# A two-layer transformer step on one core: the first chunks behind each later norm multiply an operand without the token's factor

## The chip, the cores and the metric

The kernel runs on one core of a Trainium2 chip. The metric is the device time of one execution in microseconds; 2365.01 us is the median of three runs before the change. A change of 2% of that is 47 us.

## The reference

One step of a backbone with two layers. Two groups of 128 tokens, a prompt and a sample, go through the same weights, so the kernel works on 256 token columns. Every layer has a mixer and a gated feed-forward part with a convolution over positions, each behind a norm whose output is modulated:

```python
for l in range(DEPTH):
    mod = silu(cond) @ w_ada[l] + b_ada[l]
    sh1, sc1, gt1, sh2, sc2, gt2 = split(mod, 6)
    h = rmsnorm(x, g_norm_mix[l]) * (1 + sc1) + sh1
    m = mixer_ab(h, ...) if l % 2 == 0 else mixer_c(h, ...)   # h @ w_in, attention, @ w_out
    x = x + gt1 * m
    h = rmsnorm(x, g_norm_ffn[l]) * (1 + sc2) + sh2
    x = x + gt2 * conv_ffn(h, w_ffn_up[l], ...)               # h @ w_up, conv, silu, @ w_down
return rmsnorm(x, g_final), ...

def rmsnorm(x, g):
    return x * rsqrt(mean(x * x, axis=-1) + EPS) * g
```

The norm divides every token by one factor of that token, taken over all 2048 features. The scale `(1 + sc) * g` and the shift `sh` belong to a feature and a group. So `h @ W` can also be written as the token's factor times `(x * scale) @ W`, plus `sh @ W`.

## The kernel before, in words

x lies in SBUF with the features on the partitions: 16 pieces (`KD`) of 128 features by 256 tokens. A product is computed in chunks of 128 output features. `gemm` (L330) runs one chunk: for each of the 16 blocks k three matmuls of a rounded float32 type, high weights by high operand, high weights by low operand, low weights by high operand, 128 by 128 by 256, summed in one PSUM bank. The operand lies as two halves of 256 columns, high part and rest, in one tile `hx`. The weights come as 1 MB tiles per chunk of 16 blocks; `split` (L243) makes the high part with a cast on ScalarE (L244) and the rest with a subtraction on VectorE (L245). There are three buffers for tiles, four for eight split blocks each, and three PSUM banks for sums (`pacc`).

Four norms stand ahead of products; this text is on the three later ones, ahead of the up-projection of layer 0, the input projection of layer 1 and the up-projection of layer 1. In the prediction they are seams A, B and C. Ahead of each runs a product whose chunks are added to x by `residual` (L653, L656 on VectorE): the output projection of layer 0, the second half of the down-projection of layer 0 (chunks of 22 blocks), the output projection of layer 1. Each residual is squared on ScalarE (L196) and added up on GpSimd (L200).

At the seam `modulated` (L613) does this in order. `stat_rstd` (L220) sums the squares over the features with four small matmuls, VectorE adds epsilon (L208), GpSimd raises to -0.5 (L211). `diagonal` (L231) and `spread` (L235) bring the factor to all partitions with one matmul against ones. `modulate` (L583) makes the operand in 16 pieces: x times factor on VectorE (L596), scale and shift of one group on VectorE (L602) and of the other on ScalarE (L605), the cast to the high half on ScalarE (L606), the rest on VectorE or GpSimd (L591). With `fixed` (seams B and C) this order is pinned and every fourth rest goes to VectorE, otherwise every second. `first_three` (L309) then runs three chunks at once while the pieces come, with an interleaved order of matmuls. The chunks behind them run one by one.

The modulation vectors themselves are products with `w_ada`, spread over the whole run in units of 512 outputs: row units on TensorE (`sum_rows`, L463, four groups of matmuls from four `araw` tiles of 1 MB), side units on VectorE (`sum_block`, L481, sixteen steps of two instructions from `block` tiles of 256 KB) and feature units on VectorE (L452). The lists `ROWS` and `BESIDE` say which unit goes where, `RATE`, `SIDE` and `FRATE` how many steps follow each chunk (`pump`, L553). In seam A, B and C one row unit is done within the seam. `ada_finish` (L389) turns the sums into columns.

Instructions that `keep_order` names are pinned to the order in the program; a planner places the others by its own costs. DMAs are issued by SyncE in one queue.

## Time and profile before

| | us |
|---|---|
| median of three runs | 2365.01 |
| lowest, highest | 2364.16, 2393.71 |
| profiled execution | 2362.85 |
| its span in the profile | 2361.1 |
| TensorE busy | 2306.7 (98%) |
| VectorE busy | 1847.8 (78%) |
| ScalarE busy | 1164.5 (49%) |
| GpSimd busy | 175.7 (7%) |

PE is TensorE's matmuls, PEld its weight loads, DVE VectorE, ACT ScalarE, POOL GpSimd, SP SyncE, whose queue issues the DMAs. A row of a timeline gives start and duration in us, engine, line and operation, output and inputs by the names of the program, shape and count, and in brackets the idle time before it with what ended it. A row of groups gives, behind the shape and the count, the busy time in us, the mean of one in ns, and the idle time before them. A float32 matmul that is not of the rounded type leaves two records.

### The profile page before, as it was taken

The numbers are of one execution on the slowest core, as the hardware profiler recorded it, in microseconds if no ns is written. First come the engines' busy times: TensorE is split into PE (matmuls) and PEld (weight loads), VectorE is DVE, ScalarE is ACT, GpSimd is POOL, SyncE is SP. The second block draws the span as 40 slices with busy tenths as digits, with TensorE's granted clock in tenths as the row PEclk, the third lists the DMA queues.
The fourth block names the chain that finished last, engine by engine and source line by source line (L and its number), as shares of the span: only waits on it lengthen the run. The fifth ranks groups of instructions, "written<-read, shape, count | busy, mean of one in ns | idle before, by whom it ended". The sixth has DMA issues, their size and how long they took to land. (4 is left out here: it accounts for less than half of the span.)

```text
span 2361.1 us, 47623 instructions
## 1 busy us (share of the span) xinstructions
PE 2306.7 (98%) x19624; PEld 2183.2 (92%) x19624; DVE 1847.8 (78%) x2822; ACT 1164.5 (49%) x1857; POOL 175.7 (7%) x210
## 2 busy tenths in 40 slices
PE   6999999999999999999999999999999999999997
PEld 4778768899999999999989999998999999999997
DVE  3569866779999999999878888798899755666654
ACT  4245544465553355554464444446555534555543
POOL 0002202100000000001220000022000000000011
PEclk9999999999999999999999999999999999999999
DMA  9988888667777877777768888777677555555553
GB/s 368 360 310 283 310 316 328 248 241 251 261 265 285 303 268 260 262 259 274 285 249 279 306 295 312 249 242 271 245 260 258 198 194 197 197 195 191 192 193 124
DMA packets 108249, 612.96 MB, mean 260 GB/s; under 512 B 11712, under 2 KB 19584, under 8 KB 40832
## 3 DMA queue, kind: packets, MB, share of 16 engines
q1 hardware_dynamic: 108032, 609.92, 71.3%
q8 instruction: 154, 2.52, 0.4%
q14 instruction: 63, 0.52, 0.1%
HBM read 605.12 MB, written 4.75 MB: 258 GB/s over the span
## 5 line engine op out<-in xcount | busy, mean ns | idle before, releaser
L104 PE MATMUL acc<-hx,wh 128*128 128x256 f32 x8416 | 1456.3, 278 | 9.3 <-ACT hx L606 4.4
L104 PEld LDWEIGHTS acc<-hx,wh 128*128 128x128 f32 x8416 | 1272.6, 188 | 46.8 <-issue 16.6
L244 ACT CAST wh<-raw 128x1024 fp32r<-128x1024 f32 (+1 forms) x822 | 795.3, 978 | 943.1 <-PE acc L104 759.7
L245 DVE TENSOR_TENSOR wl<-raw,wh 128x1024 fp32r<-128x1024 f32 (+1 forms) x822 | 923.8, 1141 | 315.6 <-ACT wh L244 310.4
L104 PE MATMUL acc<-hx,wl 128*128 128x256 f32 x4208 | 1167.6, 278 | 2.5 <-DVE wl L245 2.3
L104 PEld LDWEIGHTS acc<-hx,wl 128*128 128x128 f32 x4208 | 790.7, 188 | 20.1 <-issue 7.1
L104 PE MATMUL acc<-g,wh 128*128 128x256 f32 x2816 | 478.8, 276 | 0.0
L104 PEld LDWEIGHTS acc<-g,wh 128*128 128x128 f32 x2816 | 423.4, 188 | 0.0
L104 PE MATMUL acc<-g,wl 128*128 128x256 f32 x1408 | 388.0, 276 | 0.0
L452 DVE CUSTOM_DVE_ANT_0 junk<-araw,condb 128x2048 f32<-128x2048 f32 x120 | 274.7, 2289 | 0.0
L104 PEld LDWEIGHTS acc<-g,wl 128*128 128x128 f32 x1408 | 264.2, 188 | 0.0
L481 DVE SCALAR_TENSOR_TENSOR aacc<-block,condw,aacc 128x512 f32<-128x512 f32 x270 | 199.0, 769 | 9.3 <-DMA block<-w_ada 9.0
L200 POOL TENSOR_TENSOR sqacc<-sqacc,sq 128x256 f32<-128x256 f32 x62 | 91.3, 1472 | 1507.6 <-issue 1210.6
L1127 ACT ACTIVATE cv<-acc,convw 128x256 f32<-128x256 f32 x176 | 98.2, 558 | 5.1 <-PE acc L104 5.1
L104 PE MATMUL acc<-oall,wh 128*128 128x256 f32 x512 | 90.3, 281 | 1.8 <-DVE oall L245 1.1
L104 PE MATMUL ada<-araw,condw 128*32 128x512 f32 (+1 forms) x608 | 77.4, 591 | 13.6 <-DMA araw<-w_ada 13.0
L656 DVE SCALAR_TENSOR_TENSOR x<-acc,mod,x 128x128 f32<-128x128 f32 x192 | 58.1, 343 | 39.6 <-PE acc L104 39.6
L1130 DVE SCALAR_TENSOR_TENSOR cv<-acc,convw,cv 128x254 f32<-128x254 f32 x176 | 83.6, 475 | 6.1 <-ACT cv L1127 6.1
L1133 DVE SCALAR_TENSOR_TENSOR cv<-acc,convw,cv 128x254 f32<-128x254 f32 x176 | 84.4, 479 | 3.6
L104 PEld LDWEIGHTS acc<-oall,wh 128*128 128x128 f32 x512 | 78.4, 191 | 2.7 <-DVE oall L245 1.3
L104 PE MATMUL acc<-oall,wl 128*128 128x256 f32 x256 | 71.4, 280 | 0.0
L196 ACT ACTIVATE sq<-x 128x256 f32<-128x256 f32 x75 | 31.0, 415 | 36.2 <-DVE x L656 32.4
(194 smaller groups left out, 1273.7 us busy)
## 6 DMA issues: line engine op xcount, KB each, us to landing
raw<-w_up SPq DMA_DIRECT2D x176, 1024.0 KB, 4.8
araw<-w_ada SPq DMA_DIRECT2D x142, 1024.0 KB, 5.8
raw<-w_down SPq DMA_DIRECT2D x88, 1024.0 KB, 4.8
raw<-w_in_c SPq DMA_DIRECT2D x48, 1024.0 KB, 6.6
block<-w_ada SPq DMA_DIRECT2D x144, 256.0 KB, 5.2
raw<-w_in_ab SPq DMA_DIRECT2D x19, 1024.0 KB, 6.1
raw<-w_out_ab SPq DMA_DIRECT2D x16, 1024.0 KB, 7.4
raw<-w_out_c SPq DMA_DIRECT2D x16, 1024.0 KB, 6.9
```

Of the source, the lines that this page charges most:

```text
L104: return self.placed(nc.tensor.matmul(*a, **kw))
L196: act.activation(sq, src, AF.Square)
L200: eng.tensor_tensor(out=st["acc"], in0=st["acc"], in1=sq, op=ALU.add)
L244: pin(act.copy(out_hi, src))
L245: pin(dve.tensor_tensor(out=out_lo, in0=src, in1=out_hi.bitcast(F32), op=ALU.subtract))
L452: keep_order(dve.tensor_tensor_reduce(out=T_(feat["pool"], [P, D], "junk"), in1=feat["row"][:, c], in0=feat["raw"].rearrange("p g n -> p ( ...
L481: i = dve.scalar_tensor_tensor(out=acc[c], in0=block, scalar=condw[:, k, c:c + 1], in1=acc[c], op0=ALU.mult, op1=ALU.add)
L656: dve.scalar_tensor_tensor(out=x[:, c, s], in0=ps[:, s], scalar=mod[:, l, 3 * which + 2, c, g:g + 1], in1=x[:, c, s], op0=ALU.mult, op1=AL ...
L1127: pin(act.activation(y, ps, AF.Identity, scale=cw[:, 1, m:m + 1], bias=cw[:, 3, m:m + 1]))
L1130: pin(dve.scalar_tensor_tensor(out=y3[:, :, 1:], in0=p3[:, :, :T - 1], scalar=cw[:, 0, m:m + 1], in1=y3[:, :, 1:], op0=ALU.mult, op1=ALU.add))
L1133: pin(dve.scalar_tensor_tensor(out=y3[:, :, :T - 1], in0=p3[:, :, 1:], scalar=cw[:, 2, m:m + 1], in1=y3[:, :, :T - 1], op0=ALU.mult, op1=A ...
```

## The change

At the three later norms the first chunks no longer wait for the token's factor.

- While x is completed, `raw_rows` writes x times the scale, high part and rest, into a second operand tile `u`. The shift of the two groups stands beside them as two more columns (`raw_shift`), so a row is 258 wide (`UW`).
- `modulated` runs three chunks on `u`. The statistics run in the middle of chunk 0, the spread early in chunk 1, the four groups of row sums in chunks 1 and 2. `scaled` multiplies a chunk's sums in PSUM by the factor and adds the shift's column.
- The modulated operand `hx` is still made, for all later chunks, between chunk 0 and chunk 3.
- At seam C there is no row unit any more: unit (1, 5, 0) goes to the side units, (1, 3, 3) from these to the row units of the attention stage, and a fourth chunk runs on `u`, in the bank `misc`. The side units of layer 1 begin in head 0 and run at 1.4 steps per chunk of the output projection.
- `modulate` is no longer pinned. The matmuls of the chunks on `u` are.
- The operand tiles change places: seam A has `u` in a pool of its own, B and C swap between `keep` and `cc`. `o_all` moves to `keep`.

```diff
-SHIFT = 448
+SHIFT = 320
-ROWS += [(1, 2, 1), (1, 2, 2), (1, 2, 3), (1, 4, 0), (1, 3, 0)]
-ROWS += [(1, j, q) for j in (4, 3) for q in (1, 2, 3)]
+ROWS += [(1, 2, 1), (1, 2, 2), (1, 2, 3), (1, 4, 0), (1, 3, 0), (1, 3, 3)]
+ROWS += [(1, 4, 1), (1, 4, 2), (1, 4, 3), (1, 3, 1), (1, 3, 2)]
-RLIMIT = {"ab": 17, "ffn0": 21, "c": 26, "ffn1": 33}
+RLIMIT = {"ab": 17, "ffn0": 21, "c": 27, "ffn1": 33}
-BESIDE = {0: [17, 18, 19], 1: [26, 27, 28, 29, 30, 31]}
-SIDE = {"in3": 0.6, "heads": 1.05, "out0": 0.9, "c": 1.7, "outc": 2.0}
+BESIDE = {0: [17, 18, 19], 1: [27, 28, 29, 30, 31, 32]}
+SIDE = {"in3": 0.6, "heads": 1.05, "out0": 0.9, "c": 1.7, "outc": 1.4}
+UW = NT + 2
...
-    def gemm(blocks, xh, xl, n=NT, first=0, between=None):
-        fixed = lambda i: keep_order(i) if between else i
-        ps = T_(pacc, [P, 512], "acc")
+    def gemm(blocks, xh, xl, n=NT, first=0, between=None, ps=None):
+        fixed = lambda i: keep_order(i) if between is not None else i
+        ps = ps if ps is not None else T_(pacc, [P, 512], "acc")
...
-            if between and i == (last + 1) // 2:
-                between()
+            if callable(between):
+                if i == (last + 1) // 2:
+                    between()
+            elif between and i in between:
+                between[i]()
...
+    def raw_rows(u, l, which):
+        at = [0]
+        def row(c):
+            for g in range(2):
+                s = slice(g * T, (g + 1) * T)
+                act.activation(u[:, c, s], x[:, c, s], AF.Identity, scale=scl[:, l, which, c, g:g + 1])
+            for g in range(2):
+                s = slice(g * T, (g + 1) * T)
+                dve.scalar_tensor_tensor(out=u[:, c, UW + g * T:UW + (g + 1) * T], in0=x[:, c, s],
+                                         scalar=scl[:, l, which, c, g:g + 1],
+                                         in1=u[:, c, s].bitcast(F32), op0=ALU.mult, op1=ALU.subtract)
+        def behind(c):
+            for _ in range(2 if c < KD - 1 else KD):
+                if at[0] > c:
+                    break
+                if c == KD - 1:
+                    ensure(l, 3 * which + 1)
+                elif (l, 3 * which + 1, at[0] // 4) not in done:
+                    break
+                row(at[0])
+                at[0] += 1
+        return behind
...
-    def modulated(st, l, which, W, fixed):
+    def modulated(st, l, which, W, u, to):
         ensure(l, 3 * which + 1)
         ensure(l, 3 * which)
         while later:
             later.pop(0)()
+        for q in range(4):
+            raw_shift(u, l, which, q)
...
-        raws = [load_tile(0), load_tile(1)]
-        hx = T_(keep, [P, KD, ROW], "hx", F32R)
-        r = stat_rstd(st, D, att_bank)
-        sum_rows(0, raws[0], bank())
-        rb = spread(diagonal(r, (0, 1)), bank=att_bank)
-        sum_rows(1, raws[1])
-        raws += [load_tile(2), load_tile(3)]
-        modulate(hx, rb, l, which, range(KD), fixed)
...
-        ps = first_three(W, lambda k: hx[:, k, :NT], lambda k: hx[:, k, NT:2 * NT],
-                         AS_MADE if fixed else IN_TURN, lambda: sum_rows(2, raws[2]), fixed)
-        W.ahead(lambda i: i)
-        return hx, ps, [last_rows, turn]
+        def sums(t):
+            sum_rows(t, raws[t], bank() if t == 0 else None)
+            if t < 2:
+                load_tile()
+        hooks = [{8: stats}, {2: factor}, {}]
+        if unit:
+            load_tile()
+            load_tile()
+            hooks[1][8] = lambda: sums(0)
+            hooks[1][14] = lambda: sums(1)
+            hooks[2][5] = lambda: sums(2)
+            hooks[2][11] = lambda: sums(3)
+        uh, ul = (lambda k: u[:, k, :UW]), (lambda k: u[:, k, UW:])
+        ps = [gemm(W.chunk(), uh, ul, UW, between=hooks[c]) for c in range(2)]
+        last = W.chunk()
+        rb = got["rb"]
+        rbs = T_(tmp, [P, NT], "sq", bufs=2)
+        act.copy(rbs, rb)
+        hx = operand(*to)
+        for p in ps:
+            scaled(p, rbs)
+        for c in range(0, KD, 4):
+            modulate(hx, rb, l, which, range(c, c + 4))
+            if c in (4, 8):
+                W.ahead(lambda i: i)
+        ps.append(gemm(last, uh, ul, UW, between=hooks[2]))
+        scaled(ps[2], rbs)
...
+        else:
+            ps.append(gemm(W.chunk(), uh, ul, UW, between={}, ps=bank()))
+            scaled(ps[3], rbs)
+        return hx, [p[:, :NT] for p in ps], todo
+
+    def scaled(p, rb):
+        b = T_(small, [P, 2], "shift")
+        act.copy(b, p[:, NT:UW])
+        dve.tensor_tensor(out=p[:, :NT], in0=p[:, :NT], in1=rb, op=ALU.mult)
+        two = lambda v: v.rearrange("p (g t) -> p g t", g=2)
+        dve.tensor_tensor(out=two(p[:, :NT]), in0=two(p[:, :NT]),
+                          in1=b[:, :, None].to_broadcast([P, 2, T]), op=ALU.add)
...
             residual(gemm(W.chunk(), oh, ol, first=8), l, 0, c, st)
+            rows(c)
             pump(RATE["out0"] if c < KD - QUIET[1] else 0)
...
+            if h == 0:
+                side_start("c", BESIDE[1], cp, True)
...
                     residual(ps, l, 1, c, st if q == NQ - 1 else None)
+                    if rows:
+                        rows(c)
```

More of the change, by code (lines that the diff above doesn't have):

```diff
@@ L406, in copy @@
             n = NT if on_dve else 512
-            am = T_(tmp, [P, 512], "am", bufs=1)
+            if acc is None:
+                am = T_(tmp, [P, 512], "am", bufs=1)
+            else:
+                am = T_(side["pool"], [P, NT], "amside", bufs=1)
             act.copy(am[:, :n], got["ps"][:, :n])
@@ L611, in modulate, with raw_shift, home, operand @@
             low(c, h)
-    def modulated(st, l, which, W, fixed):
+    def raw_rows(u, l, which):
[20 more added lines that the diff above has]
+        return behind
+    def raw_shift(u, l, which, q):
+        k = slice(4 * q, 4 * q + 4)
+        sh = mod[:, l, 3 * which, k]
+        act.copy(u[:, k, NT:UW], sh)
+        dve.tensor_tensor(out=u[:, k, UW + NT:], in0=sh, in1=u[:, k, NT:UW].bitcast(F32), op=ALU.subtract)
+    def home(pl, tag):
+        return T_(pl, [P, (KD * 2 * UW + 127) // 128 * 128], tag, F32R)
+    def operand(pl, tag):
+        return home(pl, tag)[:, :KD * ROW].rearrange("p (k n) -> p k n", k=KD)
+    def raw_tile(pl, tag):
+        return home(pl, tag)[:, :KD * 2 * UW].rearrange("p (k n) -> p k n", k=KD)
+    def modulated(st, l, which, W, u, to):
         ensure(l, 3 * which + 1)
@@ L619, in modulated @@
             later.pop(0)()
+        for q in range(4):
+            raw_shift(u, l, which, q)
         if which:
             ada["i"] += len(BESIDE[l])
-        u = ROWS[ada["i"]]
-        tile_ = lambda t: T_(wpool, [P, 4, 512], "araw", bufs=2)
-        def load_tile(t):
-            raw = tile_(t)
-            sp.dma_start(out=raw, in_=A["w_ada"][u[0], u[1], u[2], t])
-            return raw
-        raws = [load_tile(0), load_tile(1)]
-        hx = T_(keep, [P, KD, ROW], "hx", F32R)
-        r = stat_rstd(st, D, att_bank)
@@ L650, in modulated, with load_tile, stats, factor @@
-        W.ahead(lambda i: i)
-        return hx, ps, [last_rows, turn]
+        unit = ROWS[ada["i"]] if ada["i"] < len(ROWS) else None
+        raws, got = [], {}
+        def load_tile():
+            raw = T_(wpool, [P, 4, 512], "araw", bufs=2)
+            sp.dma_start(out=raw, in_=A["w_ada"][unit[0], unit[1], unit[2], len(raws)])
+            raws.append(raw)
+        def stats():
+            got["r"] = stat_rstd(st, D, att_bank)
+            got["dg"] = diagonal(got["r"], (0, 1))
+        def factor():
+            got["rb"] = spread(got["dg"], bank=att_bank)
@@ L957, in mixer_ab, with out_ab @@
                 flush()
+        return o
+    def out_ab(o, st, u):
+        l = 0
+        rows = raw_rows(u, l, 1)
         ensure(l, 2)
@@ L1096, in mixer_c @@
         ensure(l, 2)
+        u = raw_tile(cp, "hxc")
+        rows = raw_rows(u, l, 1)
         W = Weights(A["w_out_c"], KD, 1)
@@ L1135, in conv @@
                                              op0=ALU.mult, op1=ALU.add))
-                if early:
+                if early and ready:
                     W.ahead(pin)
@@ L1158, in down @@
             def down(gs, q):
+                u, rows = None, None
+                if q == NQ - 1 and l < NL - 1:
+                    u = raw_tile(keep, "hx")
+                    rows = raw_rows(u, l + 1, 0)
                 for c in range(KD):
@@ L1187, in step_kernel @@
         half_unit(0, 0, first[0], keep_order)
-        hx = T_(keep, [P, KD, ROW], "hx", F32R)
+        hx = operand(keep, "hx")
         st = stat_init()
         with tc.tile_pool(name="beside", bufs=1) as beside:
-            mixer_ab(hx, rb0, st, beside)
-        W = Weights(A["w_up"][0], KD, 1)
-        hx, ready, todo = modulated(st, 0, 1, W, False)
+            o = mixer_ab(hx, rb0, beside)
+            with tc.tile_pool(name="raw", bufs=1) as rp:
+                T_(rp, [P, SHIFT // 4], "pad")
+                u = raw_tile(rp, "u")
+                out_ab(o, st, u)
+                W = Weights(A["w_up"][0], KD, 1)
+                hx, ready, todo = modulated(st, 0, 1, W, u, (keep, "hx"))
     stage[0] = "ffn0"
     st = stat_init()
-    ffn(hx, W, ready, todo, 0, st)
+    u = ffn(hx, W, ready, todo, 0, st)
     stage[0] = "c"
@@ L1200, in step_kernel @@
         ppool["att"] = ppool["ada"]
+        T_(cp, [P, SHIFT // 4], "pad")
         W = Weights(A["w_in_c"], KD, 1)
-        hx, ready, todo = modulated(st, 1, 0, W, True)
+        hx, ready, todo = modulated(st, 1, 0, W, u, (cp, "hxc"))
         load_cw(1)
```

32 lines of the change are left out of this document (17 added, 15 removed).

## The prediction

> **What bounds the kernel now.** I read the page's first part, then TensorE's waits to find the places where it stops, then a table by stretches over those places.
>
> ```profile
> span 2361.1 us, 47623 instructions
> PE 2306.7 (98%) x19624; PEld 2183.2 (92%) x19624; DVE 1847.8 (78%) x2822; ACT 1164.5 (49%) x1857; POOL 175.7 (7%) x210
> ...
> core 0: us, PE busy (x) PEld busy (x) DVE busy (x) ACT busy (x) POOL busy (x), PEclk, DMA share, GB/s
> 455.30:485.21 29.91, 24.18 (x182) 19.21 (x182) 22.60 (x59) 19.11 (x47) 8.05 (x9) 0.94 0.56 212
> 1188.85:1217.00 28.15, 25.02 (x181) 19.34 (x179) 22.52 (x52) 19.66 (x45) 9.88 (x13) 0.94 0.71 259
> 1613.75:1643.85 30.10, 26.34 (x191) 19.86 (x191) 24.87 (x57) 20.97 (x49) 12.74 (x14) 0.94 0.70 280
> ```
>
> TensorE is busy 98% of the span, so only what it does not do can be won. The three stretches reach from the last matmul of the output projection (of down for the second) to the end of the third chunk of the next weights: seams A, B and C, one behind each later norm. Only there, and at the start and the end of the kernel, is PE's busy time well below the stretch, and the granted clock (the column behind POOL) falls to 0.94. To price them I need TensorE's full pace and what it must do there in any case.
>
> ```profile
> 1180.92 0.39 PE L104 MATMUL acc<-g,wh 128*128 128x256 f32 x2
> 1188.40 0.39 PE L104 MATMUL acc<-g,wh 128*128 128x256 f32 x2
> 1188.74 0.28 PE L104 MATMUL att<-cst,sqacc 128*128 128x1 f32 x2
> 1190.67 0.38 PE L104 MATMUL att<-cst,sq 128*128 128x1 f32 x2 [1.65 <-ACT sq L196]
> 1193.33 1.22 PE L104 MATMUL att<-diag,cst 128*128 128x256 f32 x2
> 1196.03 0.85 PE L104 MATMUL acc<-hx,wh 128*128 128x256 f32 x2 [0.38 <-ACT hx L606]
> 1206.48 1.06 PE L104 MATMUL misc<-araw,condw 128*32 128x512 f32 x8
> ```
>
> This is TensorE's timeline at seam B. From 1180.92 to 1188.40 lie 66 matmuls: 0.1133 us each, the full pace. The seam's three chunks are 144 matmuls, 16.3 us. Beside them run three groups of row sums for the modulation (four matmuls each, 1.06 us by the row at 1206.48), 3.2 us. So 19.5 us are work, and A loses 29.91 - 19.5 = 10.4 us, B 8.65, C 10.6. In C 0.64 us more is work:
>
> ```profile
> 1613.73 0.64 PE L104 MATMUL misc<-aacc,cst 128*32 128x256 f32 x8
> ```
>
> That is **29 us in all**, the ceiling of this change. The loss in B: the square of the last chunk of x, waited for until 1190.67; the factor's chain until the spread over the partitions at 1193.33; the first modulated chunk, not there before 1196.03; then TensorE follows the modulation. The other two show the same waits:
>
> ```profile
> PE att L104 <- ACT sq L196: 2.9, 1, 2.9
> PE acc L104 <- DVE cv L1133: 1.0, 1, 1.0
> ```
> ```profile
> PE att L104 <- POOL sqacc L200: 2.0, 1, 2.0
> ```
>
> The first two rows are A's, the third is C's.
>
> **The change, part by part.** It removes the wait ahead of the first chunk: chunks 0 to 2 (in C 0 to 3) multiply x times the scale, ready before the norm, and the token's factor is put to the sums. The statistics run in the middle of chunk 0, the spread early in chunk 1. All PE instructions of these chunks are pinned in this order, so whatever a hook waits for holds up every matmul behind it. I take t0 as the seam's start.
>
> *Two more columns.* 480 matmuls (ten chunks of 48) become 258 wide.
>
> ```profile
> 310.53 0.51 PE L104 MATMUL acc<-kv_in,wh 128*128 128x384 f32 x2
> 312.09 0.51 PE L104 MATMUL acc<-kv_in,wh 128*128 128x384 f32 x2
> ```
>
> Nine matmuls of 384 columns take 1.56 us here, 0.173 each; against 0.1133 that is 0.47 ns a column, so two columns cost 0.9 ns and all of them **0.45 us**. No row shows a width of 258 or a start off a round address. Lower bound 0 (more columns give no gain); upper bound the row at 1193.33, a float32 product not rounded, 1.15 us until the next start: 480 x 1.04 = 500 us. I take the 384-wide row, which has the type of these matmuls.
>
> *Raw rows.* Per seam 32 ACT scalings and 32 DVE subtractions of 128x128, issued behind the residuals of the stage before.
>
> ```profile
> L656 DVE SCALAR_TENSOR_TENSOR x<-acc,mod,x 128x128 f32<-128x128 f32 x192 | 58.1, 343 | 39.6 <-PE acc L104 39.6
> L605 ACT ACTIVATE nt<-nt,mod,scl 128x128 f32<-128x128 f32 x64 | 29.6, 489 | 14.9 <-DVE nt L596 13.3 <-DVE mod L377 1.5
> L845 DVE TENSOR_TENSOR proj<-proj,acc 128x256 f32<-128x256 f32 x44 | 17.9, 417 | 24.4 <-PE acc L104 24.4
> L1130 DVE SCALAR_TENSOR_TENSOR cv<-acc,convw,cv 128x254 f32<-128x254 f32 x176 | 83.6, 475 | 6.1 <-ACT cv L1127 6.1
> ```
>
> By the nearest rows that is 32 x 0.489 = 15.6 us of ACT and 32 x 0.343 = 11 us of DVE. Whether they hide is read from the stages that get them (out projection, down, out projection of layer 1):
>
> ```profile
> 372.00:455.30 83.30, 83.18 (x713) 75.50 (x713) 60.06 (x93) 34.98 (x53) 19.80 (x14) 1.00 0.82 303
> 1068.50:1188.85 120.35, 120.35 (x1065) 120.35 (x1063) 106.97 (x131) 53.58 (x74) 24.63 (x14) 1.00 0.72 268
> 1518.70:1613.75 95.05, 93.26 (x803) 91.99 (x801) 87.81 (x138) 42.75 (x75) 23.37 (x18) 0.98 0.74 245
> ```
>
> DVE is idle for 23, 13 and 7 us of them, ACT for 48 or more. In the third, side sums move out: their number stays (six units of 16 steps, one exchanged for another), but they begin two products earlier at 1.7 steps each and then run at 1.4 instead of 2.0 per chunk, so of some 26 steps 96 - 44 x 1.7 = 21 stay.
>
> ```profile
> L481 DVE SCALAR_TENSOR_TENSOR aacc<-block,condw,aacc 128x512 f32<-128x512 f32 x52 | 43.4, 853 | 0.0
> ```
>
> 52 instructions in 43.4 us make 1.7 us a step, 8 us less, so DVE's idle time there stays near 5 us. I book 0.5 us for these stages; bounds 0 and all of 3 x 11 us.
>
> *Start of chunk 0.* Its rows are there but the last, which follows the last residual and is wanted 45 matmuls (5.1 us) after t0. Weights: in A
>
> ```profile
> 449.98 1.14 ACT L244 CAST wh<-raw 128x512 fp32r<-128x512 f32 x2 [1.53 <-PE acc L104]
> 456.18 2.18 ACT L244 CAST wh<-raw 128x512 fp32r<-128x512 f32 x4 [4.74 <-DMA raw<-w_up]
> ```
>
> the casts up to 449.98 are before t0 = 455.3; the one at 456.18, held by a transfer, is for the third tile, wanted 12 us later. I book nothing; were it the first, 2.5 us.
>
> *Statistics and spread.* The statistics come 26 matmuls in, at t0 + 2.95. The square was there at t0 + 1.8 in B, 0.5 us late for this in A by the wait above (2.9 us), on time in C. From the first statistic on the square to the spread B took 2.66 us, while the spread is now due only 56 matmuls in, at 6.35 plus about 0.8 for the statistics: t0 + 7.2, no wait. The two hooks cost TensorE 2.0 us.
>
> *Row sums.* Four groups stand in chunks 1 and 2 of A and B, 4.24 us, work moved and not added. Tiles 2 and 3 are loaded only when sums 0 and 1 have released their buffers: issued about t0 + 11.7, used at 17.1.
>
> ```profile
> araw<-w_ada SPq DMA_DIRECT2D x142, 1024.0 KB, 5.8
> ```
>
> With 5.8 us to land that is 0.4 us late; it hides behind the next part. In C the fifth unit moves into the attention stage, where its four groups cost the same 4.24 us.
>
> *Chunk 3 still needs the modulated operand.* This sets the seam's end.
>
> ```profile
> 1192.55 0.48 DVE L231 TENSOR_SCALAR diag<-cst,rr 128x128 f32<-128x128 f32 x2 [0.81 <-POOL rr L211]
> 1194.59 0.42 DVE L596 TENSOR_TENSOR nt<-x,att 128x256 f32<-128x256 f32 x1 [1.56 <-PE att L104]
> 1213.69 0.74 POOL L591 TENSOR_TENSOR hx<-nt,hx 128x256 fp32r<-128x256 f32 x1 [0.66 <-ACT hx L606]
> ```
>
> In B the factor was used first 1.26 us after the spread began; in the new order that is t0 + 8.4. The modulation then took from 1194.59 to 1214.43, 19.84 us. What filled it:
>
> ```profile
> L602 DVE TENSOR_SCALAR nt<-nt,scl,mod 128x128 f32<-128x128 f32 x16 | 8.4, 522 | 0.5
> L605 ACT ACTIVATE nt<-nt,mod,scl 128x128 f32<-128x128 f32 x16 | 7.9, 492 | 4.4 <-DVE nt L596 4.4
> L596 DVE TENSOR_TENSOR nt<-x,att 128x256 f32<-128x256 f32 x16 | 6.6, 413 | 1.6 <-PE att L104 1.6
> L245 DVE TENSOR_TENSOR wl<-raw,wh 128x512 fp32r<-128x512 f32 x6 | 3.9, 681 | 0.0
> ```
>
> DVE's groups come to 18.9 us with six weight splits (3.9), ACT's activation alone to 7.9 and its cast to nearly as much: the modulation is a chain over both engines that can't be compressed much. Now two splits fewer fall into it (-1.3), but the convolution of chunk 0 (2 x 0.475, not in B) and two scalings of PSUM with two instructions each (nearest row the 0.417 us add from PSUM: 0.83 each). The last of the 16 pieces is ready at 8.4 + 19.84 - 1.3 + 0.95 + 1.67 = t0 + 29.5. TensorE ends chunk 2 at 16.3 + 2.0 + 4.24 = 22.55 and wants that piece at 27.65. It waits 1.9 us, and chunk 3 ends at **t0 + 29.9**. Before, chunk 3 ended 5.44 us of matmuls and one group of sums behind the window: 36.4 in A, 34.65 in B. The gains are **6.5 and 4.75 us**.
>
> In C four chunks run ahead (24.4 us with the hooks and the 0.64). One more scaling and a split (0.65 x 2) shift the last piece to about 31.6; chunk 4 ends at 32.0, with the moved sums and the 0.64 booked 36.9, where before it was 30.10 + 1.06 + 10.88 = 42.0. Gain **5.1 us**. The sum is 16.35 - 0.45 - 0.5 = **15.4 us**. The profiled execution took 2362.85 us beside its span of 2361.1, so it would take 2347.45; the median of the runs, 2365.01, lies 2.2 us higher, so the forecast is **2349.5 us**.
>
> The granted clock may matter here: three windows of about 29 us at 0.94 are worth 1.7 us each, though no recorded wait exceeds 2.9 us. The Trainium skill, "TensorE: Matmul & The Clock Gate", section "What's actually happening", gives half rate after one idle window of about 3.4 us. By it the remaining waits of 2 us would cost no clock, as in my sum; by the rows a wait of 1.65 us among thin matmuls was enough in B, and the sum would fall by up to 5 us.
>
> **The rivals.**
>
> *Clean (17%).* The modulation keeps pace because its order is free and half of its last steps go to each of DVE and POOL. Then chunk 3 ends at 28.0 in A and B and chunk 4 at 34.1 in C: gains 8.4 + 6.65 + 7.9 - 0.45 = 22.5, **2342.5 us**. Against it: DVE and ACT fill B's window.
>
> *PSUM takes the place of the norm (17%).* Three accumulators hold chunks 0 to 2; the next chunk needs chunk 0 scaled and convolved. These instructions stand behind the modulation in the program. If they are also run there, chunk 3 of A starts at about t0 + 31 and ends at 36.5 (gain 0), chunk 4 of C at 43.4 with the moved sums (-1.4); B empties its sums by ACT and keeps its 4.75. Gain 3, **2362 us**. For it: A's wait of 1.0 us for a convolution.
>
> *Slower: the raw rows come ahead of weight splits (13%).* DVE pays 0.69 us per row in front of the splits that feed TensorE. It decides where a stage's DVE has less slack than its 11 us, which C's comes near. If every row is seen, 33 us against 15.4: **2382.6 us**.
>
> *258 columns don't run at the rounded type's pace (3%).* By the upper bound 2365 + 500 = **2865 us**.
>
> **How the numbers follow.** The forecast has 50% (2346 to 2353). From 2340 to 2366 lie that, most of the clean case, the PSUM case and the mild end of the slow one: about 82%. Two per cent, about what a measurement of this kernel can tell from no change, is 47 us: more than the 29 that there are to win, and more than the slow rival costs. So faster by over 2% gets 0.01, slower 0.03 (the last rival), within 2% 0.96.
>
> **What would show it.** Right: at t0 no wait of TensorE, the first matmul on x times the scale within 1 us of it; granted clock about 1.00 in the seams; the wait in chunk 3 (C: 4) on the modulated operand, 2 us; 258-wide matmuls at 0.114 us; DVE busy 11 us more in the stages before. Wrong: a wait on a convolution or a scaling ahead of chunk 3 or 4; waits on weight splits inside out projection or down; a hook that holds the pinned matmuls for the square, or for an araw tile, by more than 1 us.

## The result: 8 us slower, where 15 us less had been forecast

| | before | after |
|---|---|---|
| median | 2364.44 us (22 runs) | 2372.71 us (22 runs) |
| lowest, highest | 2361.22, 2393.71 | 2368.76, 2424.22 |
| profiled execution | 2362.85 | 2369.62 |

The ratio is 1.0066, with a 95% interval of 1.0044 to 1.0087. The forecast was 2349.5 us and its range ended at 2366: the sign was wrong, and the time lies outside the range, though within the 2%. Times of this kernel also jump by some 26 us at once (9 of the 22 runs after lie near 2397 or 2424, one of the 22 before at 2394), by a second pace of TensorE that the last section shows; without these runs the medians are 2364.31 and 2371.79 us, 7.5 us apart.

Counting the same matmuls in both traces gives where the change came in. The products stand in the same order, so matmul number k of one answers to number k of the other. A stretch of a seam reaches from the last matmul of the product ahead of it to the last one of the sixth chunk behind it.

| stretch | forecast, us | measured, us |
|---|---|---|
| up to seam A | 0 | -3.1 |
| seam A | -6.5 | -0.9 |
| seam B | -4.75 | +1.5 |
| attention and output projection of layer 1, with the moved unit | +4.24 | +4.6 |
| seam C | -9.3 | +4.2 |

The first row is scatter: 2.9 of its 3.1 us lie ahead of the stage that makes the raw rows of A, where no work was changed, and the product matmul at that mark (number 1512 of the list) starts between 324.2 and 328.6 us in the seventeen traces of this study. The stage with the moved unit comes out near its forecast. The three seams do not. (C's forecast is its gain of 5.1 with the moved 4.24 counted apart.)

The first part of the page and a table by stretches, both of the kernel after:

```profile
span 2367.8 us, 47881 instructions
PE 2311.2 (98%) x19624; PEld 2192.5 (93%) x19624; DVE 1881.7 (79%) x2960; ACT 1194.8 (50%) x1980; POOL 151.6 (6%) x202
...
core 0: us, PE busy (x) PEld busy (x) DVE busy (x) ACT busy (x) POOL busy (x), PEclk, DMA share, GB/s
369.10:452.40 83.30, 83.30 (x717) 75.99 (x715) 72.31 (x127) 45.46 (x87) 14.11 (x14) 1.00 0.77 288
452.38:475.99 23.61, 23.61 (x189) 19.44 (x187) 19.77 (x55) 16.33 (x42) 5.74 (x7) 1.00 0.71 266
475.99:479.66 3.67, 0.00 (x1) 0.03 (x1) 3.67 (x12) 3.63 (x9) 0.88 (x2) 0.88 1.03 404
479.66:485.55 5.89, 5.89 (x27) 5.89 (x28) 5.05 (x10) 4.46 (x11) 1.62 (x2) 0.50 0.96 380
1066.00:1184.64 118.64, 118.64 (x1049) 118.64 (x1048) 114.22 (x163) 61.61 (x108) 17.48 (x14) 1.00 0.74 270
1184.64:1209.30 24.66, 23.69 (x191) 19.65 (x190) 20.52 (x54) 17.34 (x45) 4.54 (x5) 1.00 0.87 310
1517.30:1615.90 98.60, 97.82 (x827) 93.25 (x825) 88.49 (x159) 53.42 (x109) 21.21 (x18) 1.00 0.75 259
1615.90:1620.67 4.77, 0.10 (x2) 0.02 (x2) 4.77 (x11) 1.88 (x5) 0.00 (x0) 0.81 0.53 206
1620.67:1629.10 8.43, 7.52 (x35) 6.08 (x35) 3.21 (x10) 0.61 (x2) 0.71 (x1) 0.50 0.35 124
1654.31:1659.90 5.59, 5.59 (x26) 5.55 (x27) 5.00 (x11) 5.04 (x11) 1.91 (x2) 0.51 0.78 284
```

PE's share of the span is as before, and so little help. The stretches tell it. The rows 369.10 and 1066.00 are the stages that make the raw rows of A and B: 83.30 us as before, and no idle time of PE in either; DVE is busy for 12 and 7 us more there (forecast 11). Seam A begins as drawn up, 23.61 us without an idle moment at full clock. Then PE stands still for 3.67 us, with DVE and ACT busy throughout, and behind that the clock is at 0.50 for 5.89 us. In C the stop comes ahead of everything (1615.90), the clock is low for 8.43 us, and it happens again at 1654.31.

TensorE's timeline at A, B and C:

```profile
452.38 0.49 PE L105 MATMUL acc<-u,wh 128*128 128x258 f32 x2
456.58 0.40 PE L105 MATMUL acc<-u,wh 128*128 128x258 f32 x2
459.82 0.40 PE L105 MATMUL acc<-u,wh 128*128 128x258 f32 x2
475.71 0.28 PE L105 MATMUL acc<-u,wl 128*128 128x258 f32 x1
479.66 0.77 PE L105 MATMUL acc<-hx,wh 128*128 128x256 f32 x2 [3.67 <-ACT wh L245]
...
1203.16 1.07 PE L105 MATMUL misc<-araw,condw 128*32 128x512 f32 x8 [0.97 <-DMA araw<-w_ada]
1214.79 0.38 PE L105 MATMUL acc<-hxc,wh 128*128 128x256 f32 x1 [1.24 <-DVE hxc L599]
1218.20 0.39 PE L105 MATMUL acc<-hxc,wh 128*128 128x256 f32 x1 [2.27 <-DVE hxc L599]
...
1620.67 0.59 PE L105 MATMUL att<-cst,sq 128*128 128x1 f32 x2 [4.67 <-ACT sq L197]
1625.09 0.78 PE L105 MATMUL acc<-hxc,wh 128*128 128x258 f32 x2
1654.31 0.76 PE L105 MATMUL acc<-hx,wh 128*128 128x256 f32 x2 [3.75 <-ACT wh L245]
```

VectorE's and ScalarE's timelines around these waits:

```profile
479.04 0.47 DVE L1230 SCALAR_TENSOR_TENSOR cv<-acc,convw,cv 128x254 f32<-128x254 f32 x1
...
1207.78 0.85 DVE L758 TENSOR_TENSOR rope<-dev,cst 64x256 f32<-64x256 f32 x2
1211.24 1.22 DVE L246 TENSOR_TENSOR wl<-raw,wh 128x1024 fp32r<-128x1024 f32 x1
1212.71 0.57 DVE L1074 SCALAR_TENSOR_TENSOR nlam<-ex 128x1 f32<-128x1 f32 x1
1213.20 0.87 DVE L486 TENSOR_SCALAR aacc<-block,condw 128x512 f32<-128x512 f32 x2
1218.75 0.41 DVE L599 TENSOR_TENSOR hxc<-nt,hxc 128x256 fp32r<-128x256 f32 x1
...
1616.45 0.61 DVE L633 SCALAR_TENSOR_TENSOR hxc<-x,scl,hxc 128x128 fp32r<-128x128 f32 x2
1616.97 1.28 DVE L246 TENSOR_TENSOR wl<-raw,wh 128x512 fp32r<-128x512 f32 x2
1618.18 1.40 DVE L489 SCALAR_TENSOR_TENSOR aacc<-block,condw,aacc 128x512 f32<-128x512 f32 x2
1619.51 0.60 DVE L743 SCALAR_TENSOR_TENSOR x<-acc,mod,x 128x128 f32<-128x128 f32 x2
1653.68 0.48 DVE L1230 SCALAR_TENSOR_TENSOR cv<-acc,convw,cv 128x254 f32<-128x254 f32 x1
```
```profile
467.76 1.14 ACT L245 CAST wh<-raw 128x512 fp32r<-128x512 f32 x2
478.44 1.13 ACT L245 CAST wh<-raw 128x512 fp32r<-128x512 f32 x2
1620.20 0.42 ACT L197 ACTIVATE sq<-x 128x256 f32<-128x256 f32 x1
```

*A.* The trace puts the 3.67 us down to the cast that ended at 479.57. That cast is for chunk 4; chunk 3's own weights had been cast by 468.90. The convolution of chunk 0 on DVE ended at 479.51, and only then is a bank free for chunk 3. The name in brackets is a neighbour in time; the first experiment tests this.

*B.* There is no convolution here, and the three raw chunks ran through but for 0.97 us at a tile of row sums (1203.16). Then PE waited 1.24 and 2.27 us on the modulated operand, whose last piece came at 1218.75 + 0.41, 34.5 us behind the seam's start at 1184.65. Among the modulation stands work of the next stage: the rotation of head 0 (L758), lambda (L1074), the side sums' beginning (L486) and a split of later weights (L246).

*C.* The four statistics matmuls are not inside chunk 0: they and two later groups stand ahead of it, and chunk 0 starts at 1625.09. The square they wait for is of the last residual. The product ended at 1615.9, but DVE did that residual at 1619.51, behind raw rows, a weight split and side sums. Chunk 4's wait at 1654.31 is A's over again: the convolution ended at 1653.68 + 0.48, and TensorE went on 0.15 us later, as in A.

### The profile page after: what moved, and what is told of

It is laid out like the page before. It is cut to its first block, busy times and chain, and to the rows that moved or that the text cites. A ratio compares the mean times of both kernels' runs of the same rounds, so it can differ in the third digit from the quotient of the medians.

```text
span 2367.8 us, 47881 instructions
## 1 busy us (share of the span) xinstructions
PE 2311.2 (98%) x19624; PEld 2192.5 (93%) x19624; DVE 1881.7 (79%) x2960; ACT 1194.8 (50%) x1980; POOL 151.6 (6%) x202
## 3 DMA queue, kind: packets, MB, share of 16 engines
HBM read 605.12 MB, written 4.75 MB: 258 GB/s over the span
## 4 chain that ended last, share of the span: by engine, by line
PE 91%; DVE 5%; ACT 1%; DMA 1%; issue 1%; POOL 0%; SPq 0%; DVEq 0%; ACTq 0%
PE acc L105 83%; PE ada L105 3%; PE att L105 2%; DVE wl L246 2%; PE att L108 1%; PE misc L105 1%; DVE aacc L489 1%; DMA araw<-w_ada 1%; DVE nt L604 1%; ACT wh L245 1%; DVE nt L610 0%; DMA raw<-w_in_ab 0%; PE ada L108 0%; DVE hx L599 0%; DMA block<-w_ada 0%
## 5 line engine op out<-in xcount | busy, mean ns | idle before, releaser
L105 PE MATMUL acc<-hx,wh 128*128 128x256 f32 (+1 forms) x7264 | 1258.7, 278 | 11.9 <-ACT wh L245 7.7
L246 DVE TENSOR_TENSOR wl<-raw,wh 128x1024 fp32r<-128x1024 f32 (+1 forms) x824 | 918.3, 1130 | 305.1 <-ACT wh L245 299.8
L105 PEld LDWEIGHTS acc<-hx,wh 128*128 128x128 f32 x7264 | 1100.5, 189 | 44.1 <-issue 18.7
L105 PE MATMUL acc<-hx,wl 128*128 128x256 f32 (+1 forms) x3632 | 1006.3, 278 | 2.5 <-DVE wl L246 2.3
L105 PEld LDWEIGHTS acc<-hx,wl 128*128 128x128 f32 x3632 | 683.9, 189 | 7.8 <-DVE wl L246 3.5
L105 PE MATMUL acc<-hxc,wh 128*128 128x256 f32 (+1 forms) x1536 | 271.5, 280 | 3.7 <-DVE hxc L599 3.5
L105 PEld LDWEIGHTS acc<-hxc,wh 128*128 128x128 f32 x1536 | 235.8, 190 | 4.9 <-DVE hxc L599 3.9
L105 PE MATMUL acc<-hxc,wl 128*128 128x256 f32 (+1 forms) x768 | 219.3, 286 | 0.0
L201 POOL TENSOR_TENSOR sqacc<-sqacc,sq 128x256 f32<-128x256 f32 x62 | 73.1, 1179 | 1509.6 <-issue 1194.1
L105 PEld LDWEIGHTS acc<-hxc,wl 128*128 128x128 f32 x768 | 146.2, 190 | 12.0 <-issue 6.7
```

The costliest lines, as they stand in the source:

```text
L105: return self.placed(nc.tensor.matmul(*a, **kw))
L201: eng.tensor_tensor(out=st["acc"], in0=st["acc"], in1=sq, op=ALU.add)
L246: pin(dve.tensor_tensor(out=out_lo, in0=src, in1=out_hi.bitcast(F32), op=ALU.subtract))
```

## The experiments

Theories beforehand: **bank** (chunk 3 waits for a free accumulator), **full** (VectorE has no room for the raw rows at C) and **next** (work of the next stage delays B's modulation). Against them stood the trace's own names (weights' casts), the order of the side sums, and the width of 258.

### Bank: the convolution of chunk 0 inside the modulation

```diff
     for c in range(0, KD, 4):
         modulate(hx, rb, l, which, range(c, c + 4))
+        if c == 0 and which:
+            early.append(taps(T_(tmp, [P, NT], "diag", bufs=1), ps[0], 0))
```

> The changed kernel, with the convolution of chunk 0 issued at seams A and C behind the first quarter of the modulation and not behind chunk 2 (C: 3). Theory 'accumulator': the first modulated chunk waits for that convolution to give its PSUM bank back; the waits of 3.67 us (A) and 3.75 us (C) go, with them the half clock behind each, chunk 3 (C: 4) then follows the last pieces of the modulation with waits under 2 us; 4 to 6 us less per seam, 2362 to 2365 us against 2372.7. Rival 'weights': the trace names the cast of weights as the releaser; no cast is moved, so the waits stay above 3 us and the time at 2371 to 2374 us.

Measured: 2372.66 us, ratio 1.0073 (1.0033 to 1.0112). Chunk 3 of A now starts right behind chunk 2, without the 3.67 us and at full clock, though no cast was moved: the bank was the cause. In C the wait of 3.75 us shrank to 0.77 and 1.59 us, the clock stayed at 1.00, and the seam is 2.6 us shorter in the traces. But in A the gain was lost a few matmuls later. TensorE's and VectorE's timelines of this kernel:

```profile
487.28 0.58 PE L105 MATMUL acc<-hx,wh 128*128 128x256 f32 x1 [3.92 <-DVE hx L599]
```
```profile
480.96 1.52 DVE L246 TENSOR_TENSOR wl<-raw,wh 128x512 fp32r<-128x512 f32 x2
484.13 1.55 DVE L246 TENSOR_TENSOR wl<-raw,wh 128x512 fp32r<-128x512 f32 x2
485.68 1.21 DVE L246 TENSOR_TENSOR wl<-raw,wh 128x1024 fp32r<-128x1024 f32 x1
487.41 0.41 DVE L599 TENSOR_TENSOR hx<-nt,hx 128x256 fp32r<-128x256 f32 x1
```

Three rows of splits for chunks 4 and 5 stand ahead of the last quarter of the operand. One wait was put in the place of the other.

### Full: the side sums in another order

```diff
-SIDE = {..., "c": 1.7, "outc": 1.4}
+SIDE = {..., "c": 1.7, "outc": 2.0}
```

> The changed kernel, with the side sums of the out projection of layer 1 at 2.0 steps per product in place of 1.4. Theory 'side sums': at 1.4 they run into the last product, DVE reaches the last residual late, TensorE waits 4.67 us for its square and runs at half clock behind that; at 2.0 they end two or three products before the end, the wait falls under 2 us, the clock stays up: 5 to 8 us less, 2365 to 2368 us. Rival 'raw rows': the 32 subtractions alone fill DVE, the lateness stays (wait above 3 us) or comes back as waits on weight splits inside the projection: 2371 to 2374 us.

Measured: 2396.44 us, ratio 1.0086 (1.0049 to 1.0123). In C the wait for the square fell from 4.67 to 1.47 us, and one of 2.56 us for the side sums appeared. From the end of the output projection's third chunk to the end of the sixth chunk behind C it took 130.0 us, against 130.2: no gain. What was moved came back elsewhere. That fits an engine without room: in the kernel after, DVE is busy for all 75.90 us from 1540.00 to the product's end at 1615.90.

### Next: lambda ahead of the seam, head 0's rotation behind chunk 3, side sums from head 1

```diff
+        nlam = lam_c(cp)
         W = Weights(A["w_in_c"], KD, 1)
...
+                held.append(finish)       # copies and rope of head 0, behind its products
+                if h:
+                    held.pop()(lambda i: i)
```

> The changed kernel, with work of the attention stage kept out of seam B: the lambda (an exponential with its table load) ahead of the seam, the copies and the rotation of head 0's q and k behind chunk 3, side sums from head 1. Theory 'next stage's work': these 3 us of DVE and 3 us of ACT stand inside the modulation and make its last piece late (t0 + 34.5 us, forecast 29.5); without them it is there at t0 + 31, the waits of 1.24 and 2.27 us fall under 1.5 us together and chunk 3 keeps the full clock: 3 to 5 us less, 2368 to 2370 us. Rival 'weight splits and scalings': those of chunks 4 and 5 stay inside, less than 1 us, 2372 us.

Measured: 2376.49 us, ratio 1.0081 (1.0046 to 1.0116). B got 2.7 us better (start to end of chunk 3 33.4 us, against 36.1), with waits of 1.39, 1.10 and 0.34 us left. Since the side sums began later, more of them fell to the end of the output projection, and the waits in C grew to 0.65, 4.91, 3.55 and 2.13 us. What DVE does less of early it does late.

### The seams apart: C as before, A and B changed

```diff
-        hx, ready, todo = modulated(st, 1, 1, W, u, (keep, "hx"))
+        hx, ready, todo = modulated_old(st, 1, 1, W, True)
```

with `ROWS`, `RLIMIT`, `BESIDE`, `SIDE` of before and no raw rows for C.

> The changed kernel with seam C, its raw rows and the units of the modulation as in the kernel before (the change at seams A and B alone). By the two traces aligned matmul for matmul, the attention stage, the out projection of layer 1 and seam C together lost 8.8 us: so 2363 to 2365 us if that loss is of the change at C. If A and B or the placing of tiles in memory cost it: 2370 us or more.

Measured: 2362.72 us (ten runs, 2360.02 to 2364.68), ratio 0.9990 (0.9981 to 0.9999). So the whole loss is made at C: this is 10 us below the median of the changed kernel.

### A and B mended, C as before

The first experiment's convolution and the third one's order for B, with

```diff
-            h = T_(tmp, [P, NT], "nt", bufs=4)
+            h = T_(mpool[0] or tmp, [P, NT], "nt", bufs=6 if mpool[0] else 4)
...
-            todo.append(lambda: rest[1](keep_order))
+            todo.append({5: lambda: W.ahead(keep_order), 8: lambda: rest[1](keep_order),
+                         11: lambda: W.ahead(keep_order)} if which else ...)
```

so that chunk 4's casts run inside chunk 3.

> The change at seams A and B alone (seam C as before, which took 2362.7 us), mended: in A the convolution of chunk 0 inside the modulation, the casts of chunk 4's weights inside chunk 3 and two more buffers for the modulation; in B the lambda, and the copies and rotation of head 0, out of the modulation. Theory 'what stands in front': with the accumulator freed, chunk 3 of A waited 3.92 us for the last piece of the modulation, at t0 + 33.5 us, because 4.3 us of weight splits and the convolutions stood before it on DVE; behind it they let the piece come at t0 + 29 to 30, chunk 3 ends at t0 + 31 in place of 36, no stretch at half clock: 4 to 5 us in A, 1 in B, 2356 to 2358 us. Rival 'the chain itself': DVE, ACT and POOL need this time for the modulation whatever stands beside it; last piece later than t0 + 32, 2361 us or more.

Measured: 2366.57 us, ratio 1.0029 (1.0000 to 1.0058), no better than the one above. A's chunk 3 ended 29.6 us behind the seam's start instead of 36.2, but then chunk 4 waited 2.50 us for the bank of chunk 1 and ran on at half clock (0.50), and the attention stage became 4 us longer.

### All three mended

The same with the change's C, its first convolution early, and one side unit given back to TensorE:

```diff
-BESIDE = {0: [17, 18, 19], 1: [27, 28, 29, 30, 31, 32]}
+BESIDE = {0: [17, 18, 19], 1: [28, 29, 30, 31, 32]}
```

> The changed kernel with all three seams mended (A and B as in the run beside it; in C the convolution of chunk 0 and the weights of chunk 4 ahead), and one of the six units of side sums given back to TensorE in the attention stage (4.9 us of TensorE, some 25 us less of DVE). Theory 'DVE is full': the last residual of the out projection was late because side sums, raw rows and splits together exceed what DVE can do in that stage, however they are ordered (2.0 steps in place of 1.4 won nothing); with one unit less the wait for the square falls under 1.5 us and the clock stays up: C gains 12 to 14, less 4.9, A and B 6: 2356 to 2360 us. Rival 'raw rows late by their place': the wait for the square stays above 3 us: 2364 us or more.

Measured: 2398.38 us (four runs, ratio 1.0143, 1.0128 to 1.0158), all four near 2398. The wait for the square in C fell to 0.47 us with less side work, as "full" has it; but the stage ahead of C, with two units now on TensorE, took 10.4 us more than in the kernel before, and chunk 5 waited 4.29 us, by the same reading for the bank of chunk 1 (the trace names a cast).

### The raw rows alone at C

```diff
 # on top of the kernel with C as before
+        u = raw_tile(cp, "hxc")
+        rows = raw_rows(u, l, 1)
...
             residual(product(...), l, 0, c, st)
+            rows(c)
```

> The change at A and B alone (seam C as before, 2362.7 us), with the raw rows of seam C made behind the residuals of the out projection and not used: their cost alone. By the forecast 0.2 us, hidden: 2362 to 2364 us. If DVE is full in that stage: the last residual comes 3 us late or the weight splits do, with a stretch at half clock: 4 to 8 us more, 2367 to 2371 us.

Measured: 2371.72 us (ratio 1.0046, 1.0014 to 1.0078), that is 9.0 us over the kernel without them (8.9 when each is set against the kernel before on its own chip). So one edit whose result nothing uses costs as much as the change lost at C. It was made in the old order of seam C and with 2.0 side steps per chunk, so it gives the price of the rows, not every wait of the changed kernel. The stretch from the product's end to the first chunk, in this kernel and then in the one without the rows, and the longest wait:

```profile
1615.50:1635.10 19.60, 9.80 (x41) 3.71 (x40) 17.13 (x39) 8.60 (x21) 4.40 (x5) 0.57 0.44 146
```
```profile
1609.00:1618.90 9.90, 6.96 (x33) 2.85 (x29) 6.16 (x17) 4.26 (x10) 1.56 (x2) 0.66 0.49 172
```
```profile
PE misc L105 <- DVE aacc L489: 5.0, 1, 5.0
```

DVE (the third busy time) has 17.13 us of work there instead of 6.16: 11 us more, as much as 32 subtractions take. It stands behind the product, where TensorE waits for it. The stage ahead of it took up none: from the first residual on, DVE was busy for 75.66 of 76.01 us with the rows and for 73.59 of 73.84 without them.

### Width: 256 columns, the shift left out of the raw chunks

```diff
-        uh, ul = (lambda k: u[:, k, :UW]), (lambda k: u[:, k, UW:])
+        uh, ul = (lambda k: u[:, k, :NT]), (lambda k: u[:, k, UW:UW + NT])
```

> The changed kernel with 256 columns in the chunks on the raw operand (the two columns of the shift left out, and with them the shift of these chunks). Measured so far: three matmuls of 258 columns take 0.360 us, three of 256 0.340. If the width is the cause, the chunks on the raw operand show 0.340 to 0.345; if it is the place of the operand or the engines beside it, they stay at 0.355 to 0.360. 160 groups of three: 3 us of the whole.

Measured, one execution: 2393.18 us. Three matmuls of the raw chunks still took 0.355 to 0.359 us, near the 0.357 to 0.360 with 258 columns. The width is not what costs the most.

### Statistics pinned inside chunk 0 at C, the last side sums inside chunk 1

```diff
+            hooks[1][6] = lambda: [side["then"].pop(0)() for _ in range(len(side["then"]) - 1)]
+            hooks[1][13] = lambda: side["then"].pop(0)()
...
+            hooks = [{k: pinned_(f) for k, f in h.items()} for h in hooks]
```

> The changed kernel, with TensorE's order at seam C held: the statistics in the middle of chunk 0 and the last reduction of side sums inside chunk 1, where the changed kernel ran both ahead of chunk 0. Theory 'order of TensorE': chunk 0 needs neither, so it fills the time in which the last residual and its square are late; the waits of 4.67, 0.44 and 0.47 us ahead of it shrink to one of 1 to 2 us inside it, and no half clock follows: 6 to 8 us less, 2364 to 2366 us. Rival 'DVE sets the end': the modulation and chunk 0's bank are no earlier, so chunk 4 waits for what chunk 0 won: 2370 us or more.

Measured: 2390.65 us, ratio 1.0070 (1.0025 to 1.0115); four runs at 2363.4 to 2366.6, six at 2390.5 to 2394.5. Seam C is 6.8 us shorter by the traces, and the median of the four is 7 us below that of the thirteen lower ones of the change (2364.6 against 2371.8), which supports the theory; the medians of all runs, mixed of two paces, say nothing. TensorE's timeline:

```profile
1621.78 0.38 PE L105 MATMUL att<-cst,sq 128*128 128x1 f32 x2 [1.63 <-ACT sq L197]
1649.43 0.61 PE L105 MATMUL acc<-hx,wh 128*128 128x256 f32 x2 [3.88 <-DVE cv L1243]
```

A wait of 1.63 us is left of 5.6; the bank's wait is now named rightly.

### The same, with the convolutions of chunks 0 and 1 early in A and C

```diff
+            if c == 0 and which:
+                early.append(taps(T_(tmp, [P, NT], "diag", bufs=1), ps[0], 0))
+            if c == 4 and which:
+                early.append(taps(y, ps[1], NFF))
```

with chunk 4's casts inside chunk 3 and, in A, the six buffers.

> The changed kernel with everything that the runs pointed to: TensorE's order at C held; the convolutions of chunks 0 and 1 inside the modulation (A and C), so that neither chunk 3 nor chunk 4 waits for a bank; the casts of chunk 4's weights inside chunk 3 in A, ahead in C; two more buffers for A's modulation. Theory: no wait above 2.5 us is left in A and C and the clock stays up; A 4 us, C 10 to 12 us less than the changed kernel: 2356 to 2360 us, under the kernel before. Rival 'one wait for another': the next barrier (weights of chunk 4 or 5, the modulation's last pieces) takes what is won, as twice so far: 2363 us or more.

Measured: 2369.96 us, ratio 1.0049 (1.0014 to 1.0084), six runs at 2361.9 to 2370.2, four at 2388 to 2393. A works: three waits of 0.62 us, no half clock, the last matmul of the sixth chunk 42.9 us behind the start, after the change 46.8. In C chunk 5 waits 2.02 us on ScalarE's half of the operand and 1.02 on DVE's, and half clock follows. The median of the six is no lower than that of the four above (2365.4 against 2364.6): the 3.9 us of A do not show in the sum, and I did not find where they went. Some of the runs above may have had them too, since A without this edit took 44.1 us where the clock stayed up (C as before).

### Does idle time bring the half clock? Useless matmuls in the gap

```diff
+    def idle(u):
+        d = att_bank()
+        for i in range(30):
+            keep_order(pe.matmul(d[:, :NT], u[:, 0, :T], u[:, 1, :NT], ...))
```

called ahead of the first modulated chunk of A and C.

> The changed kernel with 30 matmuls of no use (into a spare PSUM bank) between the last raw chunk and the first modulated one, at A and at C, where TensorE waits 3.67 and 3.75 us for a bank. Theory 'the idle time itself halves the clock': kept busy, TensorE runs the chunk behind at full clock, though the wait for the bank is the same: 2.7 us less at each, 2366 to 2368 us. Rival 'the clock falls for another reason': the half clock stays, the time is 2371 us or, where the matmuls come too late, more.

Measured: 2387.97 us, ratio 1.0101 (1.0040 to 1.0163). In C a wait of 1.78 us was left and no half clock followed. In A the convolution moved behind the added matmuls, a wait of 1.99 us stayed, and the half clock too. C supports the idea, A does not decide it, and in the run with 256 columns a wait of 2.49 us in A was not followed by half clock either (1.00 in the 6 us behind it).

### Rows 1056 bytes apart

```diff
+US = 264
```

`US` takes the place of `UW` in the distances; C as before.

> The change at A and B alone (seam C as before), with rows of the raw operand 264 columns apart in place of 258 (1056 bytes in place of 1032). 256 columns at 1032 bytes ran at 0.357 to 0.360 us per three matmuls, so the width is not the cause of 0.360 in place of 0.340. If the place of the rows is: 0.340 to 0.345 here. If it is something else beside these chunks: 0.360.

Measured, one execution: 2362.07 us; the raw chunks at 0.361 to 0.365 us for three. This distance does not help, then.

### A alone mended, B and C as before

The edit of the kernel with early convolutions, in A, and for B and C the code of before:

```diff
-        hx, ready, todo = modulated(st, 1, 0, W, u, (cp, "hxc"))
+        hx, ready, todo = modulated_old(st, 1, 0, W, True)
```

> The change at seam A alone (B and C as in the kernel before), mended: the convolutions of chunks 0 and 1 inside the modulation, the casts of chunk 4's weights inside chunk 3, two more buffers. From the aligned traces, up to the sixth product behind A: before 176.2 us, changed 175.1, so mended 171.2; B and C give nothing and lose nothing. Theory: 2359 to 2361 us against 2364.4. Rival: what A wins is lost again behind it (layout, a slower stretch of the attention): 2363 us or more.

Measured: **2360.29 us** (twelve runs) against 2365.12 of before on the same chip. Both have runs 26 us higher (two each), so the ratio is 0.9985 with 0.9949 to 1.0022: by medians 4.8 us faster, not clear by the interval. It is the best median of the study. How much of it is the mending is open: from the start of A to the sixth chunk this trace took 44.5 us, and the unmended A of the kernel with C as before 44.1.

### Does the last foreign instruction set the pace? Four useless transposes behind C

```diff
+                def turn4():
+                    pt = bank()
+                    for b in range(4):
+                        keep_order(pe.transpose(pt[:, b * P:(b + 1) * P], x[:, 0, :P], ident))
+                todo[1] = {8: turn4}
```

> The changed kernel with TensorE's order at C held (e9_hooks: 2363 to 2367 us in 4 of 10 executions, 2390 to 2395 in 6), and four transposes of no use in the middle of the second product behind seam C. Theory 'foreign instruction': a stretch of products keeps the pace that the instruction or stall ahead of it left; behind four transposes it was the fast one in 12 of 14 stretches, so the step of 26 us is rare: 0 to 2 of 16, median 2365 us. Rival 'not from there': still 4 to 6 of 10, median near 2390 or between.

Measured: 2366.25 us, ratio 0.9996 (0.9964 to 1.0029). One run of twelve lies 26 us higher; without the transposes it was six of ten, on another chip. This speaks for it, on twelve runs; the last section has a trace that speaks against it.

### Rows 1024 bytes apart, without the shift's columns

```diff
-UW = NT + 2
+UW = NT
```

> The changed kernel without the two columns of the shift (and so without the shift in the raw chunks), rows of the raw operand of 256 columns, 1024 bytes apart like every other operand. If the place of the rows sets the pace: 0.340 to 0.345 us per three matmuls in the raw chunks, 3 us of the whole. If something else beside these chunks does: 0.355 to 0.360 as in the two runs before.

Measured, one execution: 2408.27 us. Three matmuls of the raw chunks took 0.353 us in A and C and by turns 0.340 and 0.353 in B. These are the two paces of the last section, which other products have too. With rows 1032 or 1056 bytes apart no raw chunk kept either, so the place of the rows has a part in it, on one execution; what sets the pace stays open.

## Why the prediction was wrong, step by step

**Raw rows hidden, 0.5 us booked.** Right in two stages of three (83.30 and 118.64 us without idle time of TensorE). Wrong in C, by the largest term of the error: 9.0 us, measured by one edit. This is the step that failed. The sum over the stage counted 7 us of idle time of DVE, 15 with the side work moved out, as room for 11 us of rows. But a raw row can only be made behind a residual, and the first residual of that stage starts at 1539.32. The kernel before, ahead of that mark and behind it:

```profile
1518.70:1539.32 20.62, 18.83 (x157) 18.23 (x156) 13.56 (x27) 8.47 (x24) 1.77 (x4) 1.00 0.57 194
1539.32:1613.75 74.43, 74.43 (x648) 73.76 (x646) 74.25 (x111) 34.28 (x52) 21.61 (x14) 0.98 0.78 260
```

DVE's idle time is 7.06 us ahead of it and 0.18 behind it. Where the rows could run there was no room, so work of DVE was left over when the product ended, and the last residual, which the seam needs first, came behind part of it. The slow rival named this place; it sought the price in weight splits inside the stage, and set 33 us for all three.

**"All PE instructions of these chunks are pinned in this order."** Not so: the products are, the hooks' matmuls are not. In C the statistics ran ahead of chunk 0, so the wait that the change was made to hide stood where it had been. "The statistics come 26 matmuls in, on time in C" was wrong twice: they came first, and the square was there at 1620.62, 4.7 us behind the product's end and not by 2.95. With them and the reduction of the side sums pinned, a wait of 1.63 us is left and seam C is 6.8 us shorter. In A they did stand inside chunk 0, and on time.

**Chunk 3 waits 1.9 us on the modulated operand.** In B this was the wait, at 3.5 us. The mis-sized term is the last piece, 29.5 us from the start by forecast, 34.5 as measured: I had kept the old modulation's company (splits) and not asked what else becomes ready once chunk 0 is done early. Lambda, head 0's rotation and the side sums moved away, B got 2.7 us better. In A and C the wait was for the accumulator instead.

**PSUM takes the place of the norm (17%).** This rival came true in A and C. Its price of A was a gain of 0, measured 0.9, which is luck in part: chunk 3 started at 27.3 us and not at 31, and half clock made up the difference. I gave it too little: in the program the convolutions stand behind the modulation, and the text said so.

**258 columns, 0.45 us.** 27 matmuls take 3.24 us between the rows at 456.58 and 459.82, so three take 0.360 instead of 0.340: with 160 such groups 3.2 us. The two columns are not the main cause, since 256 took 0.355 to 0.359. Nor is 0.340 the pace throughout the old seams: stretches of all three ran at 0.353 in the kernel before.

**The granted clock.** The sum had it at 1.00. In this trace it fell to 0.50 behind the waits of 3.67, 4.67 and 3.75 us; A lost 2.8 us by it (27 matmuls in 5.89 us, at full pace 3.06), C about 6.6. By the Trainium skill, "TensorE: Matmul & The Clock Gate", section "What's actually happening", the half rate comes after an idle window of about 3.4 us. These three waits agree; but half clock also followed the 1.63 us in the kernel with pinned statistics (0.55 in the 3 us behind it).

At A the loss is a matter of the single execution. The same wait of 3.67 us stands there in eight traces. The clock behind it was 0.50 in five, 0.66 in one, and 1.00 in two: C as before, and the four transposes. In these two, A's gain in the table would be 3.7 us and not 0.9. By the same section of the Trainium skill the windows run free of what the kernel does. That would allow a wait of 3.67 us without half clock, but not half clock behind 1.63.

**Row sums.** Forecast 0.4 us late, measured 0.97 in B (1203.16) and nothing in A. The stage with the moved unit: 4.24 against 4.6. The wait at t0: none in A and B, as forecast.

## What to carry to other kernels

Work moved into "slack" must be put against the slack behind the first input that it needs, not against the stage's sum: 11 us of VectorE work hid wholly under 83 and 119 us, and cost 9 us in a stage whose idle time, 7.06 of 7.24 us, lay ahead of that input. When a wait for an operand is taken away, look for what comes next in the same place (here the accumulator, then the operand's last piece, then the next bank), and for every instruction that must run between, where the program puts it. And check in the after trace whether an order that the text calls pinned really is: the engine's own list of instructions tells it in one look.

## What was not expected of the hardware

TensorE has two paces at a granted clock of 1.00. The stretch from 1700 to 1800 us, inside one feed-forward layer, in the third experiment and in the one with pinned statistics:

```profile
1700.00:1800.00 100.00, 100.00 (x851) 100.00 (x850) 89.21 (x115) 50.91 (x72) 0.00 (x0) 1.00 0.70 254
```
```profile
1700.00:1800.00 100.00, 100.00 (x885) 100.00 (x884) 92.14 (x121) 53.99 (x75) 0.00 (x0) 1.00 0.74 269
```

851 matmuls against 885 in 100 us, 0.353 against 0.340 us for three, without a gap in either. Four more traces have a whole layer at the longer pace, 26.5 us longer than in the kernel before; that is the step of 26 us. But a layer need not keep one pace. In the run with 256 columns, products on `hx` ran at the shorter one and products on `g` (the down-projection) at the longer, in both layers, 9.4 us per layer. A stretch of `g`, then one of `hx`:

```profile
710.00:810.00 100.00, 100.00 (x851) 100.00 (x850) 89.77 (x104) 36.75 (x36) 0.00 (x0) 1.00 0.74 279
835.00:935.00 100.00, 100.00 (x884) 100.00 (x884) 92.41 (x122) 53.48 (x74) 0.00 (x0) 1.00 0.73 263
```

The pace changes with the first product on the other operand, and nothing but products runs on TensorE there. So an instruction or stall ahead of a stretch cannot be all of it.

Versions with the changed C, raw rows and new units, had the step in 38 of 80 runs (the runs without the shift and those with transposes not counted); the kernel before had it in 5 of 114, the four versions with the old C and no rows for it in 4 of 33, the one with the old C and the rows in 1 of 8. Four transposes in the stream made it one in twelve; the mechanism behind it was not found.
